# Two more seven-product couples, and two elementwise operations of each couple on GpSimd

## The chip, the cores and the metric

The kernel runs on one core of a Trainium2 chip. The core has five engines with queues of their own: TensorE (PE in the profile, its weight loads as PEld), VectorE (DVE), ScalarE (ACT), GpSimd (POOL) and SyncE (SP, which issues most of the transfers here). The metric is the device time of one execution in microseconds (us); three runs are shown for the kernel before, and a fourth one was profiled.

## The reference

The reference is a two-layer encoder trunk for 256 tokens of width 2048 in float32. Each layer adds a token mixer and then a gated MLP to the residual stream:

```python
h = h + mix                     # layer 0: bidirectional mLSTM, layer 1: bidirectional HGRN2
h = h + conv_glu(rmsnorm(h, norm_ffn_g[layer]), ffn_w_up[layer], ffn_conv_w[layer],
                 ffn_conv_b[layer], ffn_w_down[layer])
```

`conv_glu` projects 2048 to 2 x 5504, runs a width-3 convolution over the tokens on one half, and returns `(gelu(c) * v) @ w_down`, a product of 256 x 5504 by 5504 x 2048. The mixers end in a product of 256 x 2048 by 2048 x 2048 (`y @ w_out`). These two kinds of product are where the change lies. A last RMSNorm closes the trunk.

## The kernel before

*Split numbers.* TensorE multiplies in the format fp32r, which keeps fewer bits than float32. Every weight and activation is therefore split into a high part (the value cast to fp32r) and a low part (what the cast left over), and each product is made of three matmuls: high by high, high by low, low by high. The activations are split once. The weights are streamed from memory, one MB at a time, into a tile `raw` (three buffers, `RAW = 3`). `parts` then makes the high part `wh` on ScalarE (L134) and the low part `wl = raw - wh` on VectorE (L135), for up to 1024 columns at a time, into rings of four buffers each (`WB = 4`). `stream` keeps three such pieces made ahead of TensorE (`LOOK = 3`).

*Slices and couples.* The depth of a product (the contracted dimension) is cut in slices of 128. The MLP's down projection has 43 of them (5504 / 128): part 0 has the first 22, part 1 the other 21. For most products TensorE goes through all slices of one output chunk of 512 columns. The chunks of kind "st" do two output chunks at once (a *pair* of chunks) and go through the slices two by two: such a *couple* of slices is a product of 2 x 2 blocks, two token halves and two chunks, each block 128 tokens by 512 columns. `squares_by_seven` runs it. An ordinary couple needs eight block products, that is 24 matmuls of 512 columns (the loop that ends at L230). A couple listed in `ch.seven` uses the scheme of seven block products, 21 matmuls, over sums and differences of blocks. All matmuls of a pair go through `product` (L218). The seven products accumulate in C11, C12 and C21, which the ordinary couples use too (with C22), and in P1, P5, P6 and P7, which are added up once, after the last seven-product couple of the pair.

*What a seven-product couple needs besides.* The sums of the weights are made in `combine`, for the couple after the one that is being split:

```python
dve.tensor_tensor(T.rearrange("p (a b) -> p a b", a=2), B12.unsqueeze(1).broadcast_to([P, 2, 512]),
                  r[:, 0:1024].rearrange("p (a b) -> p a b", a=2), ALU.subtract)
dve.tensor_tensor(T_[:, 0:512], B22, T[:, 0:512], ALU.subtract)
dve.tensor_tensor(T_[:, 512:1024], B21, T_[:, 0:512], ALU.subtract)
```

These are L185 (1024 columns), L187 and L188 (512 each). Then each of the two 1024-column tiles is split: `th` on ScalarE (L190) and `tl` on VectorE (L191). `th` and `tl` have one buffer each. Only 512 columns of the second half of such a couple's raw weights are needed as they are, so its second `parts` is 512 wide (L135 with 512 columns). The sums of the activations, `sx`, come from `token_sums` (L514, L515), made once per couple in the up projection and used by both pairs of part 0.

*Ends of a pair.* `mid` (L527 to L535) adds P1, P5, P6 and P7 into the residual `hm` after the last seven-product couple: a copy on ScalarE, six additions on VectorE (L528 to L533), and two on GpSimd (L534, L535). `done` adds the four accumulators at the end of the pair (L540, four additions on VectorE).

*Which pairs there are.* Each layer's MLP has three: pair 1 (part 0, `w_d0`, output columns 0 to 1023), pair 2 right behind it (part 0, `w_d1`, columns 1024 to 2047), and pair 3 (part 1, `w_d0`). `mixed` makes one more per layer for the mixer's output product, with 16 slices, seven-product couples 2, 4 and 6 (`SEVEN_MIX`), and `late` set, which calls `combine` half a couple later. With `SEVEN = (1, 3, 5, 7, 9)` for pairs 2 and 3 and the first four of them for pair 1, there are 14 + 3 couples per layer, 34 in all.

*What sets the order.* The program is traced with a scheduler that places the instructions of each engine by a timeline of its own (`schedule_with_timeline_sim`). Only instructions passed through `pin` keep the written order, and these are at the start of the kernel. So the order in which VectorE and GpSimd meet these operations is the scheduler's, not the listing's. `swap` lists exchange two neighbouring matmuls of an "fm" chunk (L309 by the high part, L313 by the low part). Matmuls named `idle` run at the start while nothing else can.

Of the kernel before, what the change touches and what calls it, by code (L numbers as in the profile page):

```python
# [8 lines left out]
F32 = mybir.dt.float32  # L9
# [3 lines left out]
ALU = mybir.AluOpType  # L13
# [34 lines left out]
SEVEN = (1, 3, 5, 7, 9)  # L48
SEVEN_MIX = (2, 4, 6)

QUAD = 32
# [6 lines left out]
def trunk_kernel(ctx, tc, xT, x_d, fg_d, pp_d, cst_d, w_gate, w_first, w_aq, w_ak, w_av, w_ao, w_aout, w_ao2,  # L58
                 w_bq, w_bv, w_bg, w_bout, w_bo2, w_up, w_d0, w_d1, w_d2, out, mscr):
    nc = tc.nc  # L60
    act, dve, pool, pe = nc.scalar, nc.vector, nc.gpsimd, nc.tensor
# [9 lines left out]
    ones = keep.tile([P, T], F32, name="ones")  # L71
# [5 lines left out]
    def col(name, i):  # L77
        o = OFF[name] + i
        return pp[:, o:o + 1]
# [42 lines left out]
    pin = tc.keep_in_program_order  # L122
# [5 lines left out]

    def split_weights(chunks):

        def parts(r, m, pin=lambda ins: ins):
            wh = wpool.tile([P, 1024], F32R, tag="wh", bufs=WB, name="wh")
            wl = wpool.tile([P, 1024], F32R, tag="wl", bufs=WB, name="wl")
            pin(act.copy(wh[:, :m], r))  # L134
            pin(dve.tensor_tensor(wl[:, :m], r, wh[:, :m].bitcast(F32), ALU.subtract))  # L135
            return wh, wl

        first, loaded = chunks[0], []
        raws = first.load(loaded, chunks[1])
        for k in range(KT):  # L140
            if k == 0:
                first.x(0, pin)
            wh, wl = parts(raws[k], 512, pin)
            if k:
                first.x(k, pin)
            yield wh, wl, 1
        for ch in chunks[1:]:
            if ch.kind == "st":
                yield from split_squares(ch, parts)
                continue  # L150
            total = ch.nk * ch.width
            for b0 in range(0, total, 2048):
                b1 = min(total, b0 + 2048)
                raw = loaded.pop(0) if loaded else load_raw(ch.src, b0, b1)
                for c0 in range(0, b1 - b0, 1024):
                    m = min(1024, b1 - b0 - c0)
                    at = b0 + c0 if ch is chunks[1] else total
                    if at == 0:
                        first.gate()
                    if at < LOOK * 1024:  # L160
                        wh, wl = parts(raw[:, c0:c0 + m], m, pin)
                    elif ch is chunks[2] and b0 == c0 == 0:
                        wh, wl = parts(raw[:, c0:c0 + m], m, first.behind_v)
                    else:
                        wh, wl = parts(raw[:, c0:c0 + m], m)
                    if at == (LOOK - 1) * 1024:
                        first.sums()
                    yield wh, wl, m // ch.width

    def split_squares(ch, parts):  # L170

        units, raws, sums = (ch.nk + 1) // 2, {}, {}

        def raw(u):
            if u not in raws and u < units:
                raws[u] = load_raw(ch.src, 2048 * u, min(2048 * (u + 1), 1024 * ch.nk))
            return raws.get(u)

        def combine(u):

            r = raw(u)
            th, tl = (ch.pool.tile([P, 2048], F32R, tag=n, name=n) for n in ("th", "tl"))
            B22, B21, B12 = r[:, 512:1024], r[:, 1024:1536], r[:, 1536:2048]
            T, T_ = (ch.pool.tile([P, 1024], F32, tag="avc", bufs=2, name="T") for _ in range(2))
            dve.tensor_tensor(T.rearrange("p (a b) -> p a b", a=2), B12.unsqueeze(1).broadcast_to([P, 2, 512]),  # L185
                              r[:, 0:1024].rearrange("p (a b) -> p a b", a=2), ALU.subtract)
            dve.tensor_tensor(T_[:, 0:512], B22, T[:, 0:512], ALU.subtract)  # L187
            dve.tensor_tensor(T_[:, 512:1024], B21, T_[:, 0:512], ALU.subtract)  # L188
            for c, t in ((slice(0, 1024), T), (slice(1024, 2048), T_)):
                act.copy(th[:, c], t)  # L190
                dve.tensor_tensor(tl[:, c], t, th[:, c].bitcast(F32), ALU.subtract)  # L191
            sums[u] = th, tl

        for u in range(units):
            r = raw(u)
            if u + 1 in ch.seven and not ch.late:
                combine(u + 1)
            wh, wl = parts(r[:, 0:1024], 1024)
            yield wh, wl, 1
            if u + 1 in ch.seven and ch.late:  # L200
                combine(u + 1)
            if 2 * u + 1 < ch.nk:
                m = 512 if u in ch.seven else 1024
                wh, wl = parts(r[:, 1024:1024 + m], m)
                yield wh, wl, sums.pop(u, None)

    def squares_by_seven(ch, fetch, ready):
# [654 lines left out]
    def hgrn(norm, nxt):  # L862
# [159 lines left out]
                YT[hd] = slot(hd, "yb")  # L1022
                split(YT[hd], pz[:, 0:T], col("b_head_g", hd))

        swaps = {(0, 1): (0,), (1, 0): (2, 24), (1, 2): (4,), (2, 0): (2, 24), (2, 2): (4,), (3, 0): (2,), (3, 2): (10,)}
        heads = [dict() for _ in range(BH)]
        chunks = []
        for qd in range(BH // 4):
# [14 lines left out]
            for i in range(6):  # L1043
                if i == 3:
                    chunks.append(Chunk("tm", w_bv[qd], KT, norm.x, done_v))
                def done_i(ps, i=i, qd=qd):
                    for f in range(2):
# [3 lines left out]
                                    swap=swaps.get((qd, i), (1, 13) if i == 3 else ())))  # L1051
# [11 lines left out]
    def ffn(layer, norm, nxt):  # L1063
        stack = ExitStack()
        box = {}
        chunks, pairs = [], []

        def begin():
            box["mp"] = stack.enter_context(tc.tile_pool(name="ff", bufs=1))
            box["mp"].tile([P, LEAD], F32, name="lead")  # L1070
            for ch in pairs:
                ch.pool = box["mp"]
            if isinstance(nxt, FinalNorm):
                nxt.begin(box["mp"])

        def done_up(f, i, GT, SX):
            def go(ps):
                mp, R = box["mp"], norm.R
                avc = mp.tile([P, 1024], F32, tag="avc", bufs=2, name="avc")
                a, v, c = (avc[:, j * T:(j + 1) * T] for j in range(3))  # L1080
                fm_scaled(ps[0], R, a)
                fm_scaled(ps[1], R, v)
                cw = [col("conv_w", (layer * 3 + w) * FT + f) for w in range(3)]
                dve.tensor_scalar(c, a, cw[1], col("conv_b", layer * FT + f), ALU.mult, ALU.add)
                dve.scalar_tensor_tensor(c[:, 1:T], a[:, 0:T - 1], cw[0], c[:, 1:T], ALU.mult, ALU.add)
                dve.scalar_tensor_tensor(c[:, 0:T - 1], a[:, 1:T], cw[2], c[:, 0:T - 1], ALU.mult, ALU.add)
                act.activation(c, c, AF.Gelu)
                dve.tensor_tensor(c, c, v, ALU.mult)
                g = slot(i, "g", mp)
                act.copy(g[:, 0:T], c)  # L1090
                dve.tensor_tensor(g[:, T:2 * T], c, g[:, 0:T].bitcast(F32), ALU.subtract)
                GT.append(g)
                if i % 2 and i // 2 in SEVEN:
                    SX[i // 2] = token_sums(mp, SEVEN.index(i // 2), box["c"], c, avc[:, 0:2 * T])
                box["c"] = c
            return go

        for part, (f0, nf) in enumerate(((0, FA), (FA, FB))):
            GT, SX = [], {}
            for i in range(nf):  # L1100
                chunks.append(Chunk("fm", w_up[layer, f0 + i], KT, norm.x, done_up(f0 + i, i, GT, SX),
                                    begin if f0 + i == 0 else None,
                                    swap=(2,) if part and i == 0 else (3,) if layer and f0 + i == 1 else ()))
            def two(src, c0, norm, seven, GT=GT, SX=SX, nf=nf):
                pairs.append(pair(src, nf, c0, lambda k: GT[k], lambda u: SX[u], norm, seven))
# [14 lines left out]
    pool.memset(pad, 0.0)  # L1120
    pool.memset(pad[:, 0:4:2], 1.0)
    idle = aux("idle")
    for i in range(64):
        o = i % 4 * QUAD
        pe.matmul(idle[o:o + QUAD, 0:75], ones[:, 0:QUAD], ones[:, 0:75], start=True, stop=True)
# [115 lines left out]
```

## The time and the profile before

| | before |
|---|---|
| median of three runs | 2395.99 us (2394.94 to 2396.35) |
| the profiled execution | 2395.16 us, of which the span from first to last instruction 2393.4 |
| mean granted TensorE clock | 0.999 |
| instructions: VectorE, ScalarE, GpSimd, SyncE's 1 MB loads of `w_d` | 3141, 1987, 240, 84 |
| GpSimd busy | 186.1 us, 8% of the span |
| memory read over the span | 446.63 MB |

A row of groups gives the line of the kernel, the engine, the operation, output and inputs by their names and shapes, how many there are, the busy time of them all, the mean duration of one in ns, and after the second bar the engine's idle time just before them with what released it. A row of the timeline begins with the start and the duration in us from the first instruction; several equal instructions in line are one row, whose duration runs from the start of the first to the end of the last, and the brackets hold the idle time before it and its releaser. A row by windows gives, for a stretch of time, its length and then busy time and count for each engine. VectorE's spans include a start and an end that overlap with its neighbours in the queue, so two in line take less than twice the duration of one.

### The profile page before, as it was taken

The numbers are of one execution on the slowest core, as the hardware profiler recorded it, in microseconds if no ns is written. First come the engines' busy times: TensorE is split into PE (matmuls) and PEld (weight loads), VectorE is DVE, ScalarE is ACT, GpSimd is POOL, SyncE is SP. The second block draws the span as 40 slices with busy tenths as digits, with TensorE's granted clock in tenths as the row PEclk, the third lists the DMA queues.
The fourth block names the chain that finished last, engine by engine and source line by source line (L and its number), as shares of the span: only waits on it lengthen the run. The fifth ranks groups of instructions, "written<-read, shape, count | busy, mean of one in ns | idle before, by whom it ended". The sixth has DMA issues, their size and how long they took to land.

```text
span 2393.4 us, 37316 instructions
## 1 busy us (share of the span) xinstructions
PE 2382.4 (100%) x14592; PEld 2038.3 (85%) x14592; DVE 1898.2 (79%) x3141; ACT 1278.9 (53%) x1987; POOL 186.1 (8%) x240
## 2 busy tenths in 40 slices
PE   9999999999999999999999999999999999999998
PEld 7888888888888888888888888888888888888887
DVE  7766687777888777876898989888777788777785
ACT  7655455454544555555555555555554555455553
POOL 0100000000000000001222222220000000000000
PEclk9999999999999999999999999999999999999999
DMA  8654545555555555555445554545555555555553
GB/s 302 198 185 162 189 178 185 183 193 180 191 196 208 194 190 186 189 206 180 168 171 177 177 173 166 174 176 183 188 194 186 188 205 195 195 192 194 204 201 140
DMA packets 67680, 451.20 MB, mean 189 GB/s; under 512 B 7712, under 2 KB 8224, under 8 KB 15024
## 3 DMA queue, kind: packets, MB, share of 16 engines
q1 hardware_dynamic: 65808, 444.82, 53.4%
q0 software_dynamic: 1120, 3.21, 0.7%
q8 instruction: 114, 1.87, 0.3%
q10 hardware_dynamic: 576, 0.79, 0.1%
q14 instruction: 62, 0.51, 0.1%
HBM read 446.63 MB, written 2.16 MB: 188 GB/s over the span
## 4 chain that ended last, share of the span: by engine, by line
PE 99%; DMA 0%; ACT 0%; issue 0%; SPq 0%; DVE 0%; POOLq 0%; POOL 0%
PE mm L309 37%; PE mm L325 23%; PE mm L313 18%; PE pc L218 13%; PE mm L218 4%; PE pn L742 1%; PE py L1000 1%; PE pd L950 0%; PE pz L386 0%; PE pa L950 0%; DMA raw<-in_w_first 0%; PE S L728 0%; PE pz L1021 0%; PE pa L975 0%; PE pa L974 0%
## 5 line engine op out<-in xcount | busy, mean ns | idle before, releaser
L309 PE MATMUL mm<-xt,wh 128*128 128x512 f32 x3776 | 1317.8, 395 | 0.0
L135 DVE TENSOR_TENSOR wl<-raw,wh 128x1024 fp32r<-128x1024 f32 (+1 forms) x846 | 1012.4, 1204 | 350.5 <-ACT wh L134 341.9
L134 ACT CAST wh<-raw 128x1024 fp32r<-128x1024 f32 (+1 forms) x846 | 856.4, 1023 | 730.2 <-issue 257.0
L313 PE MATMUL mm<-xt,wl 128*128 128x256 f32 x3776 | 1048.9, 279 | 0.0
L309 PEld LDWEIGHTS mm<-xt,wh 128*128 128x128 f32 x3776 | 706.5, 188 | 161.6
L313 PEld LDWEIGHTS mm<-xt,wl 128*128 128x128 f32 x3776 | 710.3, 188 | 4.4 <-issue 0.4
L325 PE MATMUL mm<-wh,xt 128*128 128x512 f32 x1024 | 320.5, 391 | 1.1 <-ACT wh L134 0.7
L325 PEld LDWEIGHTS mm<-wh,xt 128*128 128x128 f32 x1024 | 191.4, 188 | 41.4 <-ACT xt L331 1.1
L218 PE MATMUL pc<-wh,g 128*128 128x512 f32 x648 | 211.9, 389 | 0.0
L325 PE MATMUL mm<-wl,xt 128*128 128x512 f32 x512 | 198.2, 391 | 0.0
L336 ACT COPY b<-mm 128x256 f32<-128x256 f32 x236 | 87.2, 369 | 155.9 <-PE mm L313 155.7
L218 PEld LDWEIGHTS pc<-wh,g 128*128 128x128 f32 x648 | 121.6, 188 | 25.4
L218 PE MATMUL pc<-wl,g 128*128 128x512 f32 x324 | 126.1, 389 | 0.0
L325 PEld LDWEIGHTS mm<-wl,xt 128*128 128x128 f32 x512 | 96.1, 188 | 19.0
L190 ACT CAST th<-T 128x1024 fp32r<-128x1024 f32 x68 | 70.1, 1051 | 66.8 <-PE pc L218 26.9
L337 DVE TENSOR_TENSOR avc<-mm,b 128x256 f32<-128x256 f32 x172 | 72.0, 421 | 40.6 <-ACT b L336 40.4
L534 POOL TENSOR_TENSOR hm<-hm,u 128x512 f32<-128x512 f32 x8 | 10.4, 1300 | 1181.3 <-DVE u L533 1050.8
L325 PE MATMUL mm<-wh,g 128*128 128x512 f32 x308 | 95.9, 391 | 0.0
L191 DVE TENSOR_TENSOR tl<-T,th 128x1024 fp32r<-128x1024 f32 x68 | 81.7, 1219 | 11.1 <-ACT th L190 11.1
L342 DVE TENSOR_TENSOR avc<-avc,R 128x256 f32<-128x256 f32 x172 | 72.1, 421 | 2.8
L218 PEld LDWEIGHTS pc<-wl,g 128*128 128x128 f32 x324 | 60.8, 188 | 12.4
L218 PE MATMUL mm<-th,sx 128*128 128x512 f32 x204 | 70.3, 389 | 0.0
(257 smaller groups left out, 2372.8 us busy)
## 6 DMA issues: line engine op xcount, KB each, us to landing
raw<-in_w_up SPq DMA_DIRECT2D x172, 1024.0 KB, 4.8
raw<-in_w_d SPq DMA_DIRECT2D x84, 1024.0 KB, 4.7
raw<-in_w_bq SPq DMA_DIRECT2D x48, 1024.0 KB, 4.9
raw<-in_w_ao SPq DMA_DIRECT2D x24, 1024.0 KB, 4.6
raw<-in_w_bv SPq DMA_DIRECT2D x16, 1024.0 KB, 4.6
raw<-in_w_bg SPq DMA_DIRECT2D x16, 1024.0 KB, 4.7
raw<-in_w_av SPq DMA_DIRECT2D x12, 1024.0 KB, 4.7
raw<-in_w_ak SPq DMA_DIRECT2D x8, 1024.0 KB, 4.8
```

Source lines behind the costliest of these rows:

```text
L134: pin(act.copy(wh[:, :m], r))
L135: pin(dve.tensor_tensor(wl[:, :m], r, wh[:, :m].bitcast(F32), ALU.subtract))
L190: act.copy(th[:, c], t)
L191: dve.tensor_tensor(tl[:, c], t, th[:, c].bitcast(F32), ALU.subtract)
L218: pe.matmul(ps, a, b, start=id(ps) not in begun, stop=stop and i == 2)
L309: pe.matmul(ps[f], wh[:, c:c + P], x, start=k + kk == 0, stop=False)
L313: pe.matmul(ps[f][:, 0:T], wl[:, c:c + P], x[:, 0:T], start=False, stop=k + kk == ch.nk - 1)
L325: pe.matmul(ps[t], x[:, a + t * P:a + (t + 1) * P], w[:, c], start=st and i == 0, stop=sp and i == 2)
L336: act.copy(b, ps[:, T:2 * T])
L337: dve.tensor_tensor(dst, ps[:, 0:T], b, ALU.add)
L342: dve.tensor_tensor(dst, dst, R, ALU.mult)
L742: pe.matmul(pn[:, 0:258], w, v, start=(i == 0), stop=(i == len(parts) - 1))
```

## The change

1. Pair 1 uses all of `SEVEN` in place of its first four couples, so couple 9 has seven products there too, in both layers: 36 couples in all. `pair` is called without the list.
2. In every seven-product couple, the last subtraction of weights (L188) and the 512-wide low part of the weights (the narrow L135) are issued on GpSimd in place of VectorE. `parts` takes the engine as an argument for that.
3. Two places exchange one more pair of neighbouring matmuls: position 6 in the second "fm" chunk of the HGRN2 projection, and position 3 in the second up-projection chunk of layer 0 (as layer 1 had it).
4. The idle matmuls at the start are 66 of 73 columns in place of 64 of 75.

```diff
-        def parts(r, m, pin=lambda ins: ins):
+        def parts(r, m, pin=lambda ins: ins, by=dve):
...
-            pin(dve.tensor_tensor(wl[:, :m], r, wh[:, :m].bitcast(F32), ALU.subtract))
+            pin(by.tensor_tensor(wl[:, :m], r, wh[:, :m].bitcast(F32), ALU.subtract))
...
-            dve.tensor_tensor(T_[:, 512:1024], B21, T_[:, 0:512], ALU.subtract)
+            pool.tensor_tensor(T_[:, 512:1024], B21, T_[:, 0:512], ALU.subtract)
...
-                m = 512 if u in ch.seven else 1024
-                wh, wl = parts(r[:, 1024:1024 + m], m)
+                if u in ch.seven:
+                    wh, wl = parts(r[:, 1024:1536], 512, by=pool)
+                else:
+                    wh, wl = parts(r[:, 1024:2048], 1024)
...
-        swaps = {(0, 1): (0,), (1, 0): (2, 24), ...
+        swaps = {(0, 1): (0, 6), (1, 0): (2, 24), ...
...
-                                    swap=(2,) if part and i == 0 else (3,) if layer and f0 + i == 1 else ()))
+                                    swap=(2,) if part and i == 0 else (3,) if f0 + i == 1 else ()))
...
-            chunks.append(two(w_d0[layer][:, f0 * 1024:(f0 + nf) * 1024], 0, nxt if part else None, SEVEN if part else SEVEN[:4]))
+            chunks.append(two(w_d0[layer][:, f0 * 1024:(f0 + nf) * 1024], 0, nxt if part else None))
...
-                chunks.append(two(w_d1[layer], 2, None, SEVEN))
+                chunks.append(two(w_d1[layer], 2, None))
...
-    for i in range(64):
+    for i in range(66):
         o = i % 4 * QUAD
-        pe.matmul(idle[o:o + QUAD, 0:75], ones[:, 0:QUAD], ones[:, 0:75], start=True, stop=True)
+        pe.matmul(idle[o:o + QUAD, 0:73], ones[:, 0:QUAD], ones[:, 0:73], start=True, stop=True)
```

More of the change, by code (lines that the diff above doesn't have):

```diff
@@ L1023, in finish @@
                 split(YT[hd], pz[:, 0:T], col("b_head_g", hd))
-        swaps = {(0, 1): (0,), (1, 0): (2, 24), (1, 2): (4,), (2, 0): (2, 24), (2, 2): (4,), (3, 0): (2,), (3, 2): (10,)}
+        swaps = {(0, 1): (0, 6), (1, 0): (2, 24), (1, 2): (4,), (2, 0): (2, 24), (2, 2): (4,), (3, 0): (2,), (3, 2): (10,)}
         heads = [dict() for _ in range(BH)]
@@ L1102, in ffn, with two @@
                                     begin if f0 + i == 0 else None,
-                                    swap=(2,) if part and i == 0 else (3,) if layer and f0 + i == 1 else ()))
-            def two(src, c0, norm, seven, GT=GT, SX=SX, nf=nf):
-                pairs.append(pair(src, nf, c0, lambda k: GT[k], lambda u: SX[u], norm, seven))
+                                    swap=(2,) if part and i == 0 else (3,) if f0 + i == 1 else ()))
+            def two(src, c0, norm, GT=GT, SX=SX, nf=nf):
+                pairs.append(pair(src, nf, c0, lambda k: GT[k], lambda u: SX[u], norm, SEVEN))
                 return pairs[-1]
-            chunks.append(two(w_d0[layer][:, f0 * 1024:(f0 + nf) * 1024], 0, nxt if part else None, SEVEN if part else SEVEN[:4]))
+            chunks.append(two(w_d0[layer][:, f0 * 1024:(f0 + nf) * 1024], 0, nxt if part else None))
             if part:
```

## The prediction

> **What bounds the kernel now.** I read the page's busy line, then the chain, then the stages in which the change sits, by windows.
>
> ```profile
> span 2393.4 us, 37316 instructions
> PE 2382.4 (100%) x14592; PEld 2038.3 (85%) x14592; DVE 1898.2 (79%) x3141; ACT 1278.9 (53%) x1987; POOL 186.1 (8%) x240
> PE 99%; DMA 0%; ACT 0%; issue 0%; SPq 0%; DVE 0%; POOLq 0%; POOL 0%
> raw<-in_w_d SPq DMA_DIRECT2D x84, 1024.0 KB, 4.7
> ```
>
> TensorE is busy throughout and is 99% of the chain that ended last: work removed from it is a gain in full, and every other engine costs time only where TensorE runs out of split weights. So the mean load of VectorE (79%) says little. The six stages with seven-product couples, in order (layer 0: two pairs of chunks, one pair, the 16-slice pair; layer 1: the 16-slice pair, two pairs, one pair):
>
> ```profile
> core 0: us, PE busy (x) PEld busy (x) DVE busy (x) ACT busy (x) POOL busy (x), PEclk, DMA share, GB/s
> 639.30:753.00 113.70, 113.70 (x504) 94.15 (x503) 100.56 (x113) 57.98 (x67) 3.03 (x3) 1.00 0.56 203
> 985.90:1043.00 57.10, 57.10 (x255) 47.27 (x254) 52.56 (x64) 30.34 (x36) 0.00 (x0) 1.00 0.56 199
> 323.20:364.70 41.50, 41.50 (x185) 34.37 (x184) 39.08 (x58) 22.44 (x29) 0.00 (x0) 1.00 0.54 192
> 1613.60:1655.00 41.40, 41.28 (x182) 33.89 (x181) 38.90 (x58) 23.04 (x30) 0.00 (x0) 1.00 0.51 189
> 1927.00:2041.00 114.00, 114.00 (x505) 94.36 (x504) 100.68 (x114) 58.33 (x67) 3.29 (x3) 1.00 0.56 204
> 2273.60:2331.00 57.40, 57.40 (x255) 47.41 (x254) 52.18 (x63) 30.36 (x36) 0.00 (x0) 1.00 0.56 201
> ```
>
> Here VectorE is 88 to 94% busy while TensorE never stops, but for 0.12 us in the fourth row. The clock is 1.00. A matmul of 512 columns costs 113.70 / 504 = 0.226 us. These stages decide.
>
> **The change, part by part.** *Two more couples* (couple 9 in each layer's first chunk pair): a couple issues 21 matmuls instead of 24, so 6 x 0.226 = -1.35 us. Its sums of activations are already made for the second pair and cost nothing new.
>
> *The start-up matmuls*: 66 of 73 columns for 64 of 75.
>
> ```profile
> 1.09 3.56 PE L1125 MATMUL idle<-ones 128*32 128x75 f32 x128 [1.09 <-POOL ones L1118]
> 5.34 0.50 PE L325 MATMUL mm<-wh,xt 128*128 128x512 f32 x1 [0.69 <-ACT wh L134]
> ```
>
> 4818 columns for 4800, and two instructions more (3.56 / 64 = 0.06 us each); TensorE then waits 0.69 us for ScalarE anyway: zero, and up to 0.11 if that cover were gone.
>
> *The two swaps* exchange two neighbouring matmuls; columns and weight loads stay. Each may expose or hide at most one weight load:
>
> ```profile
> L309 PEld LDWEIGHTS mm<-xt,wh 128*128 128x128 f32 x3776 | 706.5, 188 | 161.6
> L135 DVE TENSOR_TENSOR wl<-raw,wh 128x512 fp32r<-128x512 f32 x54 | 37.0, 686 | 7.9 <-ACT wh L134 7.7
> L190 ACT CAST th<-T 128x1024 fp32r<-128x1024 f32 x68 | 70.1, 1051 | 66.8 <-PE pc L218 26.9
> L191 DVE TENSOR_TENSOR tl<-T,th 128x1024 fp32r<-128x1024 f32 x68 | 81.7, 1219 | 11.1 <-ACT th L190 11.1
> L188 DVE TENSOR_TENSOR T<-raw,T 128x512 f32<-128x512 f32 x34 | 23.3, 687 | 0.4
> L534 POOL TENSOR_TENSOR hm<-hm,u 128x512 f32<-128x512 f32 x8 | 10.4, 1300 | 1181.3 <-DVE u L533 1050.8
> ```
>
> so -0.19 to +0.19 each; I take zero.
>
> *The two operations on GpSimd.* All 36 couples now put L188 and the 512-wide L135 there: 72 instructions. No DMA moves, but GpSimd becomes the last reader of a couple's weights. GpSimd needs 1.30 us for such an operation (L534), VectorE 0.69. What VectorE gives up per instruction is less than 0.69, since its instructions overlap at the ends:
>
> ```profile
> 705.23 4.10 DVE L135 TENSOR_TENSOR wl<-raw,wh 128x1024 fp32r<-128x1024 f32 x4 [1.89 <-ACT wh L134]
> 709.24 2.35 DVE L191 TENSOR_TENSOR tl<-T,th 128x1024 fp32r<-128x1024 f32 x2
> 698.94 1.81 DVE L135 TENSOR_TENSOR wl<-raw,wh 128x1024 fp32r<-128x1024 f32 x2
> 700.68 1.21 DVE L185 TENSOR_TENSOR T<-raw 128x1024 f32<-128x1024 f32 x1
> ```
>
> Two L191 take 2.35 us and the last of them 1.22 alone, so a 1024-wide one adds 1.14; the four L135 (three wide, one narrow) take 709.24 - 705.23 = 4.01, so a 512-wide one adds 0.60. The price is what GpSimd's instruction does to VectorE's while it runs. Sixteen such additions (eight L534, eight L535) are in the trace, and these show it:
>
> ```profile
> 684.73 1.30 POOL L534 TENSOR_TENSOR hm<-hm,u 128x512 f32<-128x512 f32 x1 [291.33 <-DVE u L533]
> 685.99 1.29 POOL L535 TENSOR_TENSOR hm<-hm,u 128x512 f32<-128x512 f32 x1
> 686.19 3.31 DVE L135 TENSOR_TENSOR wl<-raw,wh 128x1024 fp32r<-128x1024 f32 x2 [1.63 <-ACT wh L134]
> ...
> 367.18 1.30 POOL L534 TENSOR_TENSOR hm<-hm,u 128x512 f32<-128x512 f32 x1 [62.37 <-DVE u L533]
> 368.44 2.28 POOL L535 TENSOR_TENSOR hm<-hm,u 128x512 f32<-128x512 f32 x1
> 367.61 1.95 DVE L135 TENSOR_TENSOR wl<-raw,wh 128x1024 fp32r<-128x1024 f32 x1
> 369.48 0.67 DVE L540 TENSOR_TENSOR hm<-hm,pc 128x512 f32<-128x512 f32 x1
> 370.08 1.73 DVE L135 TENSOR_TENSOR wl<-raw,wh 128x1024 fp32r<-128x1024 f32 x1
> ```
>
> Two L135 need 3.31 us where two in line need 2.35: 0.96 us blocked, though the GpSimd instruction had already run for 0.20. So it holds VectorE for 1.16 us. At 368.44 GpSimd waits in its turn for the L135 that runs (2.28 instead of 1.30). L540, whose second input is in PSUM, is not held (0.67). So both take turns on work whose inputs are all in SBUF, and nearly all of VectorE's work here is of that kind: a moved instruction saves VectorE 0.60 us and takes 1.16.
>
> [...]
>
> *Between couples.* A normal couple and a seven-product one take TensorE 45 x 0.226 = 10.2 us. VectorE's queue holds L185, L187, three wide L135 and two L191: 6 x 1.14 + 0.60 = 7.44 us, with two GpSimd instructions 9.76. That fits, with the weights, in my layout, some 2.5 us ahead of their use: I cost it at nothing. The cover is gone if a GpSimd instruction holds VectorE for more than (10.2 - 7.44) / 2 = 1.38 us.
>
> *The seam between a layer's first and second pair.* Formerly three normal couples stood between the last seven-product couple of the first pair and the next pair; now one. VectorE meets there what was spread before: both couples' T and L191, the ten VectorE instructions of L528 to L540, and five of GpSimd's. In the built order TensorE runs pair two's couple 1 before couple 0 is through. I laid the queues out with the durations above, zero being the end of couple 10 without stalls. (1) The first matmul behind it reads a wh whose buffer couple 10 frees at -0.5; ScalarE's L134 then takes 1.05 us (as L190 of the same shape): TensorE waits 0.65. (2) VectorE ends the first L540 at +1.9, whichever GpSimd instruction runs. Then follow in its queue L531, L135, L533, L540, L185 and the L135 of couple 2: 3 x 0.60 + 3 x 1.14 = 5.2, so +7.1; TensorE asks for that last one at +7.9. But GpSimd's L135 holds L531 for 0.55, L534 holds L185 for 0.65, and L535, which waited while L185 ran, holds the L135 for 1.15: +9.5, 1.6 us late. (3) Three smaller waits there, with weight loads laid bare, 0.4 us. Together 2.7 us in each layer: +5.4. Below, none of it if the held instructions have slack that my layout lacks; above, the whole stage's sum: 100.56 + 20 x 1.16 - 18 x 0.60 + 2.9 (the new couple's own) = 115.9 us of VectorE for 113.0 of TensorE, and so for the next pair 52.56 + 10 x 0.56 = 58.2 for 57.1: at most 4.0 a layer. I take 2.7 since it is nearer to that sum.
>
> The next pair has no seam and its overshoot of 1.1 us lies behind a lead of 2 to 3 us: zero.
>
> *The 16-slice pairs* (three couples each): each moved instruction adds 1.16 - 0.60 = 0.56: 39.08 + 6 x 0.56 = 42.4 for 41.5, and 38.90 + 3.4 = 42.3 for 41.4, over by 0.9 each. Part of that VectorE can do before the stage begins; I take half, +0.9 in all, between 0 and 12 x 0.56 = 6.7.
>
> *Sum*: the profiled execution took 2395.16 us, 1.8 beside its span; -1.35 + 5.4 + 0.9 = +4.95, so 2400.1. The median of the runs shown is 0.83 higher (2395.99; 2394.94 to 2396.35); I give 2400.3, between the two.
>
> **The rivals.** *Hidden*: the seam's waits are absorbed and only the matmuls count: 2396.0 - 1.35 = 2394.6. For it: TensorE's record of 113.70 us without a gap although L534 and L535 held VectorE twice in that stage. Against: those held weights for normal couples, with slack. More cannot be gained: there is no other stall in these stages than the 0.12 us above.
>
> *Slower, in every couple*: a GpSimd instruction holds VectorE for more than 1.38 us, say 1.6 (its output is fp32r here, and two wait in line): each of 36 couples is over by 2 x 0.22 = 0.44, 16 us, less some 1 us of lead in each of 8 pairs; with seam and 16-slice pairs 2396.0 - 1.35 + 8 + 6.3 = 2409. For it: L535's 2.28 us, and 9.76 of 10.2 is full already. Against: the held time shown is 1.16.
>
> *The moved low part delays a load*: raw is freed by GpSimd, and the T of the seam's next couple stands in VectorE's queue ahead of two L135. A load takes 4.7 us; laid out, T starts 10 us before couple 10 ends, with 2 us of slack. If it is lost, some 2 us a layer more: 2404.
>
> **How the numbers follow.** Forecast (2397.5 to 2403) 0.44, hidden 0.27, every couple 0.15, late load 0.10, something else 0.04. 0.2% is 4.8 us, about what a measurement of this kernel can tell from no change: 2391.2 to 2400.8 counts as the same. The forecast lies across the upper bound, half each: slower 0.22 + 0.15 + 0.07 = 0.44; within 0.27 + 0.22 + 0.03 = 0.52; faster 0.04, since nothing of that size is there to be removed. Range: 2394.2 (hidden) to 2407 leaves out most of "every couple" and the odd rest. The forecast's own: 2397.5 to 2403.
>
> **What would show it.** GpSimd busy some 72 x 1.30 = 94 us more; L191 and the wide L135 with spreads up to 2.3 us in these stages; TensorE gaps before L218 whose releaser is VectorE's L135 or L540 in the layers' two-pair stages, about 2.7 us each, none in the one-pair stages. In the first rival those stages shrink by 0.7 us and no gap shows; in the second gaps stand in every couple. The prediction is wrong if VectorE wins the turn against a waiting GpSimd instruction, or if GpSimd's subtraction into fp32r takes longer than L534.

## The result, and the profile after

The changed kernel takes 2414.26 us (median of four runs, 2412.70 to 2414.86) against 2396.17 us before (2394.94 to 2396.45): a ratio of 1.0075, 95% interval 1.0063 to 1.0088, or +18.1 us. That is slower, and above the range that was given (2394.2 to 2407.0). The profiled execution took 2414.86 us, 1.8 beside its span.

The page of the changed kernel:

```profile
span 2413.1 us, 37377 instructions
PE 2391.4 (99%) x14590; PEld 2040.0 (85%) x14590; DVE 1923.3 (80%) x3079; ACT 1283.1 (53%) x1991; POOL 342.6 (14%) x312
PE 91%; DVE 4%; DMA 2%; issue 1%; POOL 1%; ACT 0%; SPq 0%; POOLq 0%; DVEq 0%; ACTq 0%
L135 POOL TENSOR_TENSOR wl<-raw,wh 128x512 fp32r<-128x512 f32 x36 | 87.2, 2424 | 801.3 <-ACT wh L134 801.3
L188 POOL TENSOR_TENSOR T<-raw,T 128x512 f32<-128x512 f32 x36 | 66.5, 1848 | 153.0 <-DVE T L187 137.0
```

TensorE was 99% of the chain and is 91% now. VectorE has 62 instructions fewer and is busy 25 us longer. GpSimd is busy 156 us more where 72 x 1.30 = 94 was expected: its two operations take 2.42 and 1.85 us, since they wait for their turn.

The same six stages, by windows of the changed kernel (the order is that of the prediction's table):

```profile
core 0: us, PE busy (x) PEld busy (x) DVE busy (x) ACT busy (x) POOL busy (x), PEclk, DMA share, GB/s
640.40:760.70 120.30, 115.14 (x501) 92.94 (x500) 109.05 (x98) 60.21 (x69) 47.48 (x23) 1.00 0.54 192
993.40:1050.50 57.10, 57.10 (x254) 47.26 (x253) 54.92 (x52) 30.65 (x38) 19.64 (x10) 1.00 0.58 201
324.40:365.90 41.50, 41.50 (x185) 34.38 (x184) 38.49 (x51) 22.86 (x29) 13.20 (x6) 1.00 0.55 191
1621.10:1663.60 42.50, 42.02 (x181) 33.44 (x180) 38.05 (x51) 22.98 (x29) 15.39 (x6) 1.00 0.51 175
1940.10:2060.70 120.60, 116.32 (x502) 94.47 (x501) 109.78 (x99) 60.26 (x69) 45.44 (x23) 0.99 0.55 192
2293.40:2350.80 57.40, 57.40 (x255) 47.34 (x254) 55.14 (x53) 31.11 (x37) 19.39 (x10) 1.00 0.57 200
```

The pairs that stand alone and layer 0's 16-slice pair have no gap. The two stages of two pairs have, and so has layer 1's 16-slice pair. But these are not the whole of it. The next fences are windows over the first up projection of a layer, some 1153 matmuls with no gap in any, layer 1 and then layer 0; first the kernel before, then the changed one:

```profile
1716.10:1915.80 199.70, 199.70 (x1153) 174.63 (x1152) 153.49 (x259) 101.18 (x150) 0.00 (x0) 1.00 0.56 191
424.30:628.00 203.70, 203.70 (x1154) 176.63 (x1154) 153.71 (x259) 101.47 (x150) 0.00 (x0) 1.00 0.55 187
```

```profile
1725.20:1928.60 203.40, 203.40 (x1153) 176.47 (x1152) 153.40 (x259) 101.32 (x149) 0.00 (x0) 1.00 0.56 187
425.50:629.10 203.60, 203.60 (x1154) 176.66 (x1153) 153.66 (x259) 101.47 (x150) 0.00 (x0) 1.00 0.56 187
```

The same instructions run at two paces, at a full clock and without a wait: 11.09 us a chunk, or 11.31. In the kernel before layer 1 had the quick pace and layer 0 the slow one; the change leaves both slow.

All stages can be measured between the same ScalarE copies (L336, L338 after the change) of the two traces. Where the profiled execution's 19.67 us came from: the start +1.20 (0.65 by the first copy, through a wait for the first activations that differs between executions by more than this, see the last section, and 0.55 in a stop behind it that no other run has); two-pair stage +6.56 in layer 0 and +6.57 in layer 1 (these contain the 0.68 us gained by the new couple); layer 1's first up projection +4.44; layer 1's 16-slice pair +1.24; the other parts of the kernel -0.34 together, of which -0.35 in the two chunks of HGRN2 at the new exchange.

The gaps of layer 0's seam, in the timeline of TensorE (start, duration, and in brackets the idle time and its releaser):

```profile
694.11 0.50 PE L220 MATMUL pc<-wl,g 128*128 128x512 f32 x1 [1.44 <-DVE wl L135]
...
699.44 0.50 PE L220 MATMUL mm<-wh,g 128*128 128x512 f32 x1 [0.50 <-ACT wh L134]
...
701.64 0.50 PE L220 MATMUL mm<-tl,sx 128*128 128x512 f32 x1 [1.24 <-DVE tl L191]
...
703.38 0.50 PE L220 MATMUL pc<-wh,g 128*128 128x512 f32 x1 [0.54 <-DVE hm L542]
...
710.87 0.50 PE L220 MATMUL pc<-wl,g 128*128 128x512 f32 x1 [1.45 <-DVE wl L135]
```

The second and the last are the two that I had laid out (0.65 us for a wh, 1.6 for the L135 behind the held L185; a stop costs some 0.15 us beside the idle time shown: the first is 1.60 us from start to start beyond the usual 0.23, for 1.44 of idle). The first, third and fourth I had not. What VectorE did ahead of the first, in its timeline and in GpSimd's:

```profile
678.38 1.23 DVE L185 TENSOR_TENSOR T<-raw 128x1024 f32<-128x1024 f32 x1 [1.69 <-DMA raw<-in_w_d]
679.64 0.69 DVE L187 TENSOR_TENSOR T<-raw,T 128x512 f32<-128x512 f32 x1
680.25 5.69 DVE L135 TENSOR_TENSOR wl<-raw,wh 128x1024 fp32r<-128x1024 f32 x3
685.86 2.35 DVE L191 TENSOR_TENSOR tl<-T,th 128x1024 fp32r<-128x1024 f32 x2
691.70 1.23 DVE L185 TENSOR_TENSOR T<-raw 128x1024 f32<-128x1024 f32 x1 [3.49 <-DMA raw<-in_w_d]
692.84 2.35 DVE L135 TENSOR_TENSOR wl<-raw,wh 128x1024 fp32r<-128x1024 f32 x2
```

```profile
680.46 2.16 POOL L188 TENSOR_TENSOR T<-raw,T 128x512 f32<-128x512 f32 x1 [7.14 <-DVE T L187]
682.58 2.27 POOL L135 TENSOR_TENSOR wl<-raw,wh 128x512 fp32r<-128x512 f32 x1
```

Three L135 take 5.69 us where 1.22 + 2 x 1.14 = 3.5 is usual: two of them wait for a GpSimd instruction, 1.1 us each. They are among the readers that free the raw weights, so the loads are asked for later. SyncE's rows show it: the load for couple 1 of pair 2 is issued at 683.18 us in the run with couples only (next section) and at 686.00 in the changed kernel.

```profile
683.18 0.33 SPq L126 DMA_DIRECT2D raw<-in_w_d  x1
```

```profile
686.00 0.33 SPq L126 DMA_DIRECT2D raw<-in_w_d  x1
```

Counted from the last ScalarE copy of the up projection, that is 40.4 and 44.9 us: 4.5 us later. The eight loads before it are issued 1.0 to 4.0 us later, more and more towards the seam. So VectorE stands still for 3.49 us in front of the L185 of pair 2's couple 1, whose load has not landed, and the L135 that TensorE needs for couple 10 is behind it in the queue.

### The profile page after: what moved, and what is told of

Read it like the earlier page. It is cut to its first block, busy times and chain, and to the rows that moved or that the text cites. A ratio compares the mean times of both kernels' runs of the same rounds, so it can differ in the third digit from the quotient of the medians.

```text
span 2413.1 us, 37377 instructions
## 1 busy us (share of the span) xinstructions
PE 2391.4 (99%) x14590; PEld 2040.0 (85%) x14590; DVE 1923.3 (80%) x3079; ACT 1283.1 (53%) x1991; POOL 342.6 (14%) x312
## 3 DMA queue, kind: packets, MB, share of 16 engines
HBM read 446.63 MB, written 2.16 MB: 186 GB/s over the span
## 4 chain that ended last, share of the span: by engine, by line
PE 91%; DVE 4%; DMA 2%; issue 1%; POOL 1%; ACT 0%; SPq 0%; POOLq 0%; DVEq 0%; ACTq 0%
PE mm L311 36%; PE mm L327 21%; PE mm L315 18%; PE pc L220 9%; PE mm L220 3%; DVE wl L135 2%; DMA raw<-in_w_d 1%; PE pn L744 1%; DVE tl L191 1%; POOL wl L135 1%; PE py L1002 1%; PE pd L952 0%; PE pz L388 0%; PE pa L952 0%; DVE T L185 0%
## 5 line engine op out<-in xcount | busy, mean ns | idle before, releaser
L135 DVE TENSOR_TENSOR wl<-raw,wh 128x1024 fp32r<-128x1024 f32 (+1 forms) x810 | 1022.3, 1267 | 334.0 <-ACT wh L134 325.4
L220 PE MATMUL pc<-wh,g 128*128 128x512 f32 x620 | 204.1, 391 | 0.5 <-DVE hm L542 0.5
L135 POOL TENSOR_TENSOR wl<-raw,wh 128x512 fp32r<-128x512 f32 x36 | 87.2, 2424 | 801.3 <-ACT wh L134 801.3
L338 ACT COPY b<-mm 128x256 f32<-128x256 f32 x236 | 87.2, 369 | 157.5 <-PE mm L315 157.4
L191 DVE TENSOR_TENSOR tl<-T,th 128x1024 fp32r<-128x1024 f32 x72 | 98.6, 1390 | 7.4 <-ACT th L190 7.2
L188 POOL TENSOR_TENSOR T<-raw,T 128x512 f32<-128x512 f32 x36 | 66.5, 1848 | 153.0 <-DVE T L187 137.0
L344 DVE TENSOR_TENSOR avc<-avc,R 128x256 f32<-128x256 f32 x172 | 78.0, 455 | 2.8
```

The lines of the kernel that those rows point to most:

```text
L135: pin(by.tensor_tensor(wl[:, :m], r, wh[:, :m].bitcast(F32), ALU.subtract))
L188: pool.tensor_tensor(T_[:, 512:1024], B21, T_[:, 0:512], ALU.subtract)
L220: pe.matmul(ps, a, b, start=id(ps) not in begun, stop=stop and i == 2)
L338: act.copy(b, ps[:, T:2 * T])
L344: dve.tensor_tensor(dst, dst, R, ALU.mult)
```

## The experiments

The first theory (S): the stops at the seam come from GpSimd's instructions where only one normal couple is left; the pace (P) is a state that the swaps and the arrival of the stream set. Rivals: the crowded seam alone (C); GpSimd in every couple. All runs together, in us longer than the kernel before; the stages are those of one profiled execution each, measured as above, and the medians are of 4 to 11 runs:

| run | two-pair stage, layer 0 | layer 1 | first up projection, layer 0 | layer 1 | median, us |
|---|---|---|---|---|---|
| changed kernel | +6.56 | +6.57 | -0.01 | +4.44 | 2414.26 |
| couples only | +2.83 | +4.47 | 0.00 | 0.00 | 2402.37 |
| all but GpSimd | +2.84 | +6.09 | -4.46 | 0.00 | 2400.26 |
| GpSimd only | +0.47 | +0.47 | -4.46 | +4.44 | 2398.23 |
| swaps and idle only | 0.00 | -0.03 | -4.46 | 0.00 | 2391.27 |
| changed, no swap at 3 | +5.59 | +6.34 | -4.46 | 0.00 | 2404.49 |
| changed, seam on VectorE | +6.64 | +6.99 | -0.01 | +4.44 | 2414.34 |
| changed, late mark | +7.33 | +6.14 | -0.01 | +4.44 | 2413.96 |
| all but GpSimd, late mark | +2.83 | +5.33 | -4.46 | 0.00 | 2400.49 |
| changed, pair 2 from couple 3 | +1.14 | +0.67 | -0.01 | +4.45 | 2402.65 |
| changed, L188 alone on GpSimd | +4.82 | +4.75 | -4.46 | 0.00 | 2400.40 |
| changed, narrow L135 alone on GpSimd | +1.86 | +3.18 | -0.01 | +4.44 | 2406.42 |
| all but GpSimd, L536 and L537 on VectorE | +2.78 | +4.04 | -0.01 | -1.37 | 2410.20 |

### Couples only

```diff
-SEVEN if part else SEVEN[:4]
+SEVEN
```

> The kernel before with couple 9 of pair 1 in seven products, nothing else (both operations stay on VectorE, swaps and idle matmuls as before). Theory S (the seam stalls come from GpSimd's instructions stretching VectorE's at a seam that has only one normal couple): the seam keeps its 0.65 us wait for a free wh and little else, -1.35 + 1.3 = about 2396.1 us, between 2394.6 and 2398. Rival C (the crowded seam alone does it, whoever runs the two operations): the two-pair stages each still hold some 7 us of TensorE gaps, about 2408 us.

2402.37 us, ratio 1.0029 (1.0017 to 1.0041). Neither: the seam loses 2.83 and 4.47 us, the 0.68 gained included, with no GpSimd operation added. In VectorE's timeline of this run, and TensorE's:

```profile
679.07 4.09 DVE L135 TENSOR_TENSOR wl<-raw,wh 128x1024 fp32r<-128x1024 f32 x4
684.30 2.36 DVE L191 TENSOR_TENSOR tl<-T,th 128x1024 fp32r<-128x1024 f32 x2 [1.14 <-ACT th L190]
689.24 1.23 DVE L135 TENSOR_TENSOR wl<-raw,wh 128x1024 fp32r<-128x1024 f32 x1 [2.58 <-ACT wh L134]
690.38 1.22 DVE L185 TENSOR_TENSOR T<-raw 128x1024 f32<-128x1024 f32 x1
...
703.79 2.04 DVE L191 TENSOR_TENSOR tl<-T,th 128x1024 fp32r<-128x1024 f32 x1
705.75 2.31 DVE L185 TENSOR_TENSOR T<-raw 128x1024 f32<-128x1024 f32 x1
```

```profile
709.25 0.50 PE L220 MATMUL pc<-wl,g 128*128 128x512 f32 x1 [1.33 <-DVE wl L135]
```

Here four L135 take 4.09 us, the load is there when L185 wants it, and no stop precedes couple 10. What is left is a wh (0.46 idle), another wh (0.45), and 1.33 us for an L135 behind an L191 and an L185 that the two additions of `mid` on GpSimd, which the kernel before has too, stretch to 2.04 and 2.31. Couple 9 brought VectorE's work next to those additions. So GpSimd's new operations explain about 3.7 us of the seam in layer 0, the couple the rest. In layer 1 the same difference is 2.1 us, and only 0.5 against the next run, which has the changed kernel's other edits: that layer's share is not settled.

### All but GpSimd

```diff
-            pool.tensor_tensor(T_[:, 512:1024], B21, T_[:, 0:512], ALU.subtract)
+            dve.tensor_tensor(T_[:, 512:1024], B21, T_[:, 0:512], ALU.subtract)
-                    wh, wl = parts(r[:, 1024:1536], 512, by=pool)
+                    wh, wl = parts(r[:, 1024:1536], 512)
```

> The changed kernel with both operations back on VectorE (couples, swaps and idle matmuls as changed). Theory S as for the run with couples only: no seam stalls beyond about 0.7 us. Theory P (the pace of an up projection, 11.09 or 11.31 us a chunk, is a state that the swaps and the arrival set; no GpSimd needed): layer 1's first up projection runs at 11.31 as in the changed kernel, +4.5 us, about 2400.5. Rival Q (GpSimd's stalls in the 16-slice pair just before turned that pace): it runs at 11.09, about 2396.

2400.26 us, ratio 1.0017 (1.0008 to 1.0026). The seam as with couples only, 1.6 us dearer in layer 1. Layer 1's up projection keeps 11.09, so without GpSimd's operations the swaps do not slow it: rival Q holds so far. Layer 0's has become quick; the run with the swaps alone, below, shows why.

### GpSimd only

```diff
-norm, SEVEN))
+norm, SEVEN if part or c0 else SEVEN[:4]))
```

(of the changed kernel, with the swaps and the idle matmuls of the one before)

> The move to GpSimd alone: pair 1 keeps four seven-product couples, swaps and idle matmuls as before. Theory S: three normal couples at the seam absorb the held time, so only the layer-1 16-slice pair's 1.3 us remain: about 2397.5 us if the up projections keep their pace, 2402 if GpSimd's stalls in the 16-slice pair turn layer 1's to 11.31 (rival Q). Rival C': the move costs at the seam even so, 7 us a layer: about 2411.

2398.23 us, ratio 1.0010 (1.0001 to 1.0019). The seam costs 0.47 us a layer: with three normal couples GpSimd's holding is nearly free. The paces change in both layers, -4.46 and +4.44, and cancel; layer 1's up projection is slow here with the exchange at position 3 that it had before. The move alone is worth about +2 us.

### Swaps and idle matmuls only

```diff
-        swaps = {(0, 1): (0,), ...
+        swaps = {(0, 1): (0, 6), ...
-(3,) if layer and f0 + i == 1
+(3,) if f0 + i == 1
-    for i in range(64):    # 75 columns
+    for i in range(66):    # 73 columns
```

> The kernel before with the two swaps and the 66 x 73 idle matmuls alone. My forecast's step: zero, 2396.2. Theory P: a swap turns the pace of the up projection that follows, so layer 0's first one goes from 11.31 to 11.09 a chunk (22 chunks, -4.5 us, about 2391.5) or stays, and the second chunk of the HGRN2 projection gains 0.2; and layer 1's changes only if its arrival has changed (+4.5).

2391.27 us, ratio 0.9980 (0.9971 to 0.9989), 4.9 us quicker than before and the best kernel of this study. One exchange of two neighbouring matmuls in layer 0 (position 3) makes the whole up projection that follows quick:

```profile
424.20:623.90 199.70, 199.70 (x1153) 174.57 (x1153) 153.53 (x259) 101.23 (x149) 0.00 (x0) 1.00 0.56 191
```

199.70 us for the 203.70 of the kernel before. Apart from the idle matmuls, TensorE's order differs from that of the kernel before in the two exchanges alone. The turn stands at the exchanged pair itself: up to it, the starts of the matmuls follow each other as in the kernel before (241, 120, 236, 113, 233, 117 ns, over and over), and from a few matmuls behind it (404 us) at 231, 112, 233, 117. The swap at position 6 in HGRN2 gives 0.35 us, 0.15 in its own chunk and 0.20 in the next, where nothing was changed; the idle matmuls give nothing that can be seen.

### The changed kernel without the swap at 3

```diff
-swap=(2,) if part and i == 0 else (3,) if f0 + i == 1 else ()))
+swap=(2,) if part and i == 0 else ()))
```

> The changed kernel without the swap at position 3 of the second up-projection chunk, in both layers. Theory P (a swap turns the pace of the matmuls that follow, either way; in the changed kernel both up projections arrive at 11.09 us a chunk and the swap turns them to 11.31): both first up projections run at 11.09, 22 and 21 chunks by 0.21 us, -9.1, about 2405.2 us. Rival Q (the stalls in the 16-slice pair keep the pace at 11.31 whatever the swap): layer 1 stays at 11.31, 2409.7 or 2414.

2404.49 us, as theory P had it (2405.2): both layers go to 11.09, by windows layer 1 and layer 0:

```profile
1718.70:1918.40 199.70, 199.70 (x1153) 174.63 (x1152) 153.47 (x259) 101.26 (x150) 0.00 (x0) 1.00 0.56 191
424.30:624.00 199.70, 199.70 (x1155) 174.65 (x1154) 153.65 (x259) 101.33 (x150) 0.00 (x0) 1.00 0.56 191
```

The same swap that quickens the kernel before slows the changed one. This run has every engine's instructions in the changed kernel's order but for the exchanged pair in each layer, so the swap is the cause. It turned the pace, whichever it was: from slow to quick in layer 1 of the kernel before (at 1694 us), from quick to slow in both layers of the changed one (at 403 and 1703 us); the arrival decided which way. In the changed kernel the order of the matmuls around the small transposes ahead of the up projection is another, and the stream arrives quick (230 and 117 ns in turn at 402 us, where the kernel before has 241, 120, 236). That the arrival follows from this order is argued, not shown. What the pace is within TensorE stays open: in the trace the starts of the slow one repeat after six matmuls (241, 120, 236, 113, 233, 117 ns, high and low in turn), those of the quick one after two (about 231 and 116).

### The seam's couples on VectorE

```diff
+        ch.onv = (9,) if nk == FA and c0 == 0 else (1,) if nk == FA else ()
-            pool.tensor_tensor(T_[:, 512:1024], ...
+            (dve if u in ch.onv else pool).tensor_tensor(T_[:, 512:1024], ...
-512, by=pool)
+512, by=dve if u in ch.onv else pool)
```

> The changed kernel with both operations on VectorE in the two couples at the seam alone (couple 9 of pair 1, couple 1 of pair 2), on GpSimd in the other 32. Theory S2 (couple 9 costs some 4 us a layer by itself, and GpSimd's instructions inside the seam the rest): the two-pair stages fall to what the run with couples only showed, 3.7 us less in layer 0 and 2.1 in layer 1, about 2408.5 us. Rival L (GpSimd's instructions in the couples before the seam use up VectorE's lead): no change, about 2414.

2414.34 us, no gain, as rival L had it. The loads were late before the seam began. The waits of VectorE from the start of pair 1 to the first stop at the seam (us in total, times, longest), in the changed kernel, in this run and in the run with couples only:

```profile
DVE T L185 <- DMA raw<-in_w_d: 7.0, 3, 3.5
```

```profile
DVE T L185 <- DMA raw<-in_w_d: 7.0, 3, 4.2
```

```profile
DVE T L185 <- DMA raw<-in_w_d: 0.3, 1, 0.3
```

GpSimd's operations in the couples ahead delay the readers of raw, and so the loads: that for couple 1 of pair 2 is issued 3.2 us later here than with couples only. TensorE's stock of split weights hides this until the seam.

### The late mark, with and without GpSimd

```diff
-norm, SEVEN))
+norm, SEVEN, c0 == 2))
```

> The changed kernel with pair 2 marked late as the 16-slice pairs are, so its sums of weights are asked for half a couple later. Theory W (the first seam stall, 1.60 us in layer 0 and 1.14 in layer 1, is VectorE's L135 of couple 10 behind an L185 that waits for a load): these two waits go and the others stay, 2414.3 - 2.9 = about 2411.4 us. Rival: L185 waits elsewhere or L191 comes later, no gain or some us of loss, 2414 to 2420.

> The same late mark in the kernel that has couples, swaps and idle matmuls as changed but both operations on VectorE (2400.3 us). If the order of L185 and L135 at the seam is what makes couple 9 dear even there (its 1.6 us wait for an L135 behind an L185), -1.7 in each layer and -1.6 for the clock that falls after that wait in layer 1: about 2395.3 us. If the sheer number of VectorE's instructions is, about 2400.

2413.96 and 2400.49 us. The edit is lost: the scheduler put every engine's instructions in the same order as without it. So these two say nothing on theory W. They are second measurements of 2414.26 and 2400.26, and show that the stages of one execution vary by up to 0.8 us (7.33 and 6.56 in layer 0, 5.33 and 6.09 in layer 1).

### Pair 2 from couple 3

```diff
-norm, SEVEN))
+norm, SEVEN[1:] if c0 else SEVEN))
```

> The changed kernel with couple 1 of pair 2 as an ordinary couple (pair 2 uses 3, 5, 7, 9), so that no L185 stands in VectorE's queue at the seam; GpSimd's operations stay in all others. Theory L (GpSimd's instructions delay the loads of every couple by some 2 us, and at the seam the L185 of pair 2's couple 1 waits for such a load with couple 10's low parts behind it): the seam's gaps fall from 7 to about 1 us a layer; two couples fewer cost 1.35, so 2414.3 - 12 + 1.4 = about 2403.7 us. If couple 9's own crowding and the late loads are enough without that L185, gaps of 4 us or more stay: 2409 or more.

2402.65 us, as theory L had it (2403.7). With GpSimd everywhere and couple 9 in place, but no L185 at the seam, the gaps are nearly gone; layer 0's stage by windows:

```profile
641.90:756.80 114.90, 114.45 (x504) 93.94 (x503) 104.69 (x95) 58.22 (x67) 43.95 (x21) 1.00 0.54 201
```

0.45 us of TensorE idle instead of 5.16. The seam needs both couples, the one at its end and the one behind it. This edit takes away the waiting L185 and some of VectorE's work with it; how much each of the two is worth isn't told apart.

### One operation alone

```diff
 # L188 alone: the narrow L135 back on VectorE
-                    wh, wl = parts(r[:, 1024:1536], 512, by=pool)
+                    wh, wl = parts(r[:, 1024:1536], 512)
 # the narrow L135 alone: L188 back on VectorE
-            pool.tensor_tensor(T_[:, 512:1024], ...
+            dve.tensor_tensor(T_[:, 512:1024], ...
```

> The changed kernel with the narrow L135 back on VectorE; only L188 runs on GpSimd. Theory L: half the held time per couple, so loads are asked for about 1 us later than without GpSimd, and the two-pair stages lie between the run without GpSimd (2.8 and 6.1 us longer than before) and the changed kernel (6.6 and 6.6). If the narrow L135 is the one that matters (it is needed by TensorE at once and frees the raw weights), the stages equal those without GpSimd. Pace of the up projections open, 4.5 us each: 2399 to 2410 us.

> The changed kernel with L188 back on VectorE; only the narrow L135 runs on GpSimd. The same reading as for the run with L188 alone: under theory L about as dear as that one; if the narrow L135 is the one that matters, the two-pair stages are as in the changed kernel (6.6 us longer each). 2399 to 2414 us by the pace of the up projections.

2400.40 and 2406.42 us; without the paces the order turns around: L188 on GpSimd makes the two-pair stages 4.82 and 4.75 us longer, the narrow L135 1.86 and 3.18, no more than with neither (2.84 and 6.09). In layer 0 the dear one is L188; in layer 1 neither alone is seen to cost more than none, and both together (6.57) hardly more. My second reading, that the narrow L135 matters, is refuted, and so is theory L's that both are about as dear. The loads agree in layer 0: with L188 alone those ahead of the seam are issued up to 1.5 us later than with couples only and VectorE waits 6.4 us for them; with the narrow L135 alone up to 0.7 us later, and it waits 2.3. Why L188 delays them more isn't shown. The paces part the two the other way: with the narrow L135 alone both first up projections are slow as in the changed kernel, with L188 alone they are quick.

### The two additions of mid on VectorE

```diff
-            pool.tensor_tensor(part(1, 0), part(1, 0), u, ALU.add)
-            pool.tensor_tensor(part(1, 1), part(1, 1), u, ALU.add)
+            dve.tensor_tensor(part(1, 0), part(1, 0), u, ALU.add)
+            dve.tensor_tensor(part(1, 1), part(1, 1), u, ALU.add)
```

> The kernel with couples, swaps and idle matmuls as changed, both operations on VectorE (2400.3 us), and now the two additions L536 and L537 on VectorE too: no GpSimd at the seam at all. If the 1.6 us wait of that kernel is L191 and L185 held by those two additions (2.04 and 2.31 us where 1.22 is usual), it shrinks by 2 x (1.0 - 0.6) = 0.8 us and the clock doesn't fall behind it in layer 1: 2400.3 - 1.6 - 1.6 = about 2397 us. If not, 2400.

2410.20 us: the wait of 1.33 us fell to 0.6, as said, but the stages gained only 0.06 and 2.05 us, so in layer 0 other waits took its place. The second up projections, which have one pace in all other runs, went from 11.09 to 11.31 in both layers, +4.28 each. That part has a swap of its own (position 2 of its first chunk), which no run touched. The -1.37 in the table is no gain: the ScalarE copy that begins the stage came 1.38 us later here, while TensorE's matmuls kept their times.

## Why the prediction was wrong

*Right.* The idle matmuls at about zero (TensorE's first real matmul starts at 5.45 us in place of 5.34). The matmuls saved (-0.68 a layer) are as written; no stage shows them by themselves. The price of one instruction: predicted 1.16 us of VectorE held, measured 2.32 - 1.22 = 1.10 on the wide L135s. The steady couples: no stop in any pair that stands alone, so the rival "in every couple" (2409) was rightly less likely, although the time came out beyond it. At the seam, two of the waits, at their size (0.65 for a wh, 1.6 for the L135). The 16-slice pairs: +0.9 forecast in all; layer 1's came out 1.24 longer in the changed kernel and 0.04 with the swaps alone, layer 0's 0.08 shorter. One sign of being wrong that the prediction names did occur, VectorE winning the turn against a waiting GpSimd instruction (last section), but it spares VectorE and isn't what made the time longer.

*Wrong, first: the seam, 2.7 us a layer.* Measured: 7.2 us in each layer (6.56 and 6.57 beside the 0.68 saved), 1.6 of it in layer 1 by a halved clock. The step that failed is the cover ahead of the seam. I costed the couples before it at nothing, with weights "some 2.5 us ahead", and gave the seam's L185 "2 us of slack", from a layout in which raw weights came free at their old times; the late load that would use this up I priced at 2 us a layer with a chance of 0.10 and kept apart from the forecast. The runs show the cover gone, in layer 0 most clearly: loads are issued up to 4.5 us later, VectorE waits 7.0 us for them ahead of the seam where it waited 0.2 before, and the low parts of couple 10 stand behind the last of these waits. GpSimd's instruction that holds L135 for 1.1 us also holds the load that L135 releases, and the delay goes round: reader, load, next couple's L185. The third and fourth stop (L191, then the accumulator's L542) stand behind that L185 in VectorE's queue. I had named the instruction ahead of the two L135, and not added it to the others: late load and seam were not rivals, they come together. I also put the late load down to the moved low part; alone on GpSimd that one leaves the stages no longer than with neither, and L188, which I had not suspected, is the dearer one in layer 0. In layer 1 the couple alone loses nearly as much, and how much GpSimd adds there stays open.

*Wrong, second: cost of the couple without GpSimd.* My layout put all waits but the 0.65 down to the new operations. Couples only lost 3.5 us in layer 0 (2.83 beside the 0.68 saved): 1.33 of idle at `mid`'s own two additions, which I had counted as if the new instructions were needed to make them dear, and two waits for a wh. In layer 1 it was 5.2, and 6.8 in the run without GpSimd, 1.6 of each by the halved clock. With `mid`'s additions on VectorE too, layer 0's stage gained only 0.06: the crowded queue costs this, whoever runs them.

*Wrong, third: the swaps at zero, or 0.19 us.* I priced an exchange by the weight load that it may lay bare. It turned the pace of all that followed: 4.46 us, down in the kernel before and up in the changed one. The trace of before shows it: 203.70 and 199.70 us for the same matmuls in two layers, without a wait in either. Of the profiled execution's 19.7 us this is 4.4, the two seams 13.1, layer 1's 16-slice pair 1.2.

The whole change is a sum of parts that don't add: swaps alone -4.9, GpSimd alone +2.1, couples alone +6.2 make +3.4, and together they are +18.1. Couples and GpSimd meet at the seam, and GpSimd's effect on the arrival turns the swap's gain into a loss.

## What to carry to other kernels

An instruction that holds another engine's reader also delays what this reader frees (here 1.1 us on an L135, and loads up to 4.5 us late). Follow it round the ring (reader, load, next sum of weights) for several turns before a layout says that there is slack, and count mechanisms that share a queue as a sum and not as rivals. Where TensorE is the bound, compare the time per matmul of equal stages before anything else: stages at full clock without waits can still differ by 2% (203.70 and 199.70 us here), and an edit of two instructions can turn a stage of 200 us. Measure such an edit again after every change upstream, since it has no sign of its own (-4.46 us on the kernel before, +4.45 and +4.44 on the changed one).

## What the runs showed of the hardware

*GpSimd and VectorE held each other up, mostly in turn.* In the rows above (680 to 686 us) neither gets its second instruction before the other has had one: L188 takes 2.16 instead of 1.30 us and L135 on GpSimd 2.27, while VectorE's second and third L135 take 2.32 and 2.31 instead of 1.22. But the turns weren't strict. Six of GpSimd's 36 L135 take 3.3 to 5.0 us, and here two L191 run past one that waits, 2.35 us for both as if they were alone:

```profile
699.98 3.87 POOL L135 TENSOR_TENSOR wl<-raw,wh 128x512 fp32r<-128x512 f32 x1 [2.76 <-ACT wh L134]
```

```profile
700.37 2.35 DVE L191 TENSOR_TENSOR tl<-T,th 128x1024 fp32r<-128x1024 f32 x2
```

*Some gaps of 1.29 to 2.48 us were followed by half the clock.* Layer 1's seam of the changed kernel, by windows:

```profile
1999.00:2001.80 2.80, 0.58 (x3) 0.15 (x1) 2.80 (x3) 0.09 (x1) 1.59 (x1) 1.00 0.42 97
2001.80:2003.00 1.20, 1.11 (x3) 0.92 (x4) 1.20 (x3) 0.00 (x0) 0.00 (x0) 0.57 0.99 416
2003.00:2004.00 1.00, 1.00 (x4) 0.59 (x3) 1.00 (x2) 0.00 (x0) 0.00 (x0) 0.50 0.67 279
2004.00:2005.00 1.00, 1.00 (x3) 0.79 (x3) 1.00 (x2) 0.00 (x0) 0.00 (x0) 0.50 0.00 0
```

After a gap of 2.48 us (between matmul starts, beyond the usual 0.23) the granted clock is 0.50 and a matmul takes 0.427 us instead of 0.227, for 3.41 us (3.4 with couples only): some 1.6 us lost. The length of the gap alone didn't decide. The half clock followed gaps of 1.29 us (L188 alone, layer 1), 1.38 (no swap at 3, layer 0), 1.62 (all but GpSimd, layer 1) and 1.65 (couples only, layer 1), and not one of 1.61 in layer 0 of the changed kernel nor one of 1.68 in layer 0 with L188 alone. It makes up the 1.6 us by which layer 1's seam is dearer than layer 0's with couples only, and half of the 3.25 in the run without GpSimd. What else decides is not shown.

*The first microseconds differ between executions.* TensorE waits there for the first split activations; in the profiled executions of the kernel before, the changed one and the one with couples only:

```profile
10.56 0.49 PE L325 MATMUL mm<-wh,xt 128*128 128x512 f32 x1 [0.39 <-ACT xt L331]
```

```profile
9.87 0.49 PE L327 MATMUL mm<-wh,xt 128*128 128x512 f32 x1 [1.39 <-ACT xt L333]
```

```profile
10.65 0.49 PE L327 MATMUL mm<-wh,xt 128*128 128x512 f32 x1 [2.02 <-ACT xt L333]
```

With the halved clock that follows the wait in the third (3.41 us at 0.50), this moves a single execution by up to some 3 us (1.63 us more of waiting than in the first, 1.6 by the clock), so one profile of this kernel can't settle an effect below that; the stage lengths can.
